# Token tile 0 transposed among tile 1's last matmuls, the next weights converted behind its parts

## The chip, the cores and the metric

The kernel runs on one core of a Trainium2 chip. The metric is the device time of one execution, in microseconds (us). Four engines matter here, each with a queue of its own that it works through in order: TensorE (PE in the profile, its weight loads PEld) multiplies, VectorE (DVE) and ScalarE (ACT) do element-wise work, and SyncE (SP) issues the loads from memory.

## The reference

Two transformer blocks run one after the other on 256 tokens of width 1024, all in float32. Where a block ends one sublayer and begins the next, the same steps come: a full-width projection, an addition to the residual, an RMS norm, and the next projection. Cut to that, the three places of the change are:

```python
# first block, behind the mixer and behind the feed-forward part
x = x + rms_norm(merged @ w_out, norm_mix_post)
h = rms_norm(x, norm_ffn_pre)
u = causal_dwconv(h @ w_up, conv_ffn_w)
...
x = x + rms_norm(f @ w_down, norm_ffn_post)
u = rmsnorm(x, norm_mix_g_2)          # second block begins
proj = u @ w_in_2
...
# second block, behind its mixer
h = x + merged @ w_out_2
hn = rmsnorm(h, norm_mlp_g_2)
y = square(relu(hn @ w_up_2)) @ w_down_2
```

## The kernel before

The 256 tokens lie in two tiles of 128 (`tt` is 0 or 1). A float32 product is made of three matmuls of rounded parts: every operand is split into a high part and the rest (`wh` and `wl` for weights, the two halves of an `Act` tile for activations), and `mm_N` issues high by high, high by rest, and rest by high. The conversion of a weight piece, 128 rows by 1024 numbers, is a cast on ACT (`wh<-raw`, L186) and a subtraction on DVE (`wl<-raw,wh`, L187). The raw pieces come by DMA into four buffers, so a new load is issued when the subtraction four pieces earlier is done.

The program gives an order of work; a scheduler then sets the order of instructions on each engine ahead of the run, and the engines keep to it. `tc.issue_after(i)` binds what is traced inside to stand behind instruction `i` on its engine.

The change concerns three passages from a projection with the tokens in the rows of its result to the next such projection. They are called passage 1 (`w_out` to `w_up`, activations `h2T`), passage 2 (`w_down` to `w_in_2`, `uT`) and passage 3 (`w_out_2` to `w_up_2`, `hnT`). In each:

- `down_tail` finishes the projection: PE fills two PSUM banks for tile 0, then two for tile 1 (`pN`, 48 matmuls for a tile in passages 1 and 3).
- `normed` then works on tile 0: squares of the two banks on ACT, a reciprocal root in small steps on DVE (`rsr`, `rsa` and others), the new residual `x`, its squares, and the normed tile `xm`, in two halves. `to_T` transposes it on PE (`tr`, eight transposes into two banks), and casts on ACT with subtractions on DVE split each bank into two parts of the activations. The same chain of squares, `x` and `xm` follows for tile 1.
- `head_N` multiplies the normed tiles with the first 1024 columns of the next weights, in two halves of 512 columns (`n` 0 and 1), each of four pieces of two `k` each. PE does tile 0 with half 0, tile 0 with half 1 (`pM`, 24 matmuls each), transposes tile 1, and does tile 1 with both halves.

In `head_N` the first `free` pieces of half 0 are converted when the scheduler likes, the others of half 0 behind the last square and the last half of tile 0's `xm` (`normed_`), and all of half 1 behind the last split of tile 0 (`transposed`). `free` is 2 in passages 1 and 2, and 4 in passage 3.

Of the kernel before, what the change touches and what calls it, by code (L numbers as in the profile page):

```python
# [18 lines left out]
P = 128  # L19
# [20 lines left out]
def two_blocks(ctx, tc, ins, out):  # L40
# [240 lines left out]
    def down_tail(banks, w, parts, wts, first, last=False):  # L281
# [17 lines left out]
    def head_N(w, cols, x, ready, done, free=2):  # L299
# [14 lines left out]
    def head_T(w, cols, x, ready, free=2):  # L314
# [6 lines left out]
        head_N(w, cols, x, ready, done, free)  # L321
# [62 lines left out]
    def normed(x, g, dst, mid):  # L384


        xms = []
        for tt in range(NT):
            mid(tt)
            xms.append(norm(x, tt, g))  # L390
            if tt == 0:
                split0 = to_T(dst, 0, xms[0][0])

        def ready(tt):
            if tt:
                to_T(dst, tt, xms[tt][0])

        ready.marks = xms[0][1], split0
        return ready

    def post_norm(x, tt, banks, g):
# [4 lines left out]
        for n in range(2):  # L406
            nc.scalar.activation(sq, banks[n], AF.Square, accum_out=s2[:, n:n + 1])
            nc.vector.tensor_mul(fg[:, n * 512:(n + 1) * 512], banks[n], g[:, n * 512:(n + 1) * 512])
        r = rsqrt([s2[:, 0:1], s2[:, 1:2]], 1.0 / D)
        for n in range(2):  # L410
            cs = slice(n * 512, (n + 1) * 512)
            nc.vector.scalar_tensor_tensor(x[tt][:, cs], fg[:, cs], r, x[tt][:, cs], ALU.mult, ALU.add)

# [209 lines left out]
    def proj_full_N(w, x):  # L623

        banks = [[ps("pN"), ps("pN")] for _ in range(NT)]
        down_tail(banks, w, [(k, x, k) for k in range(KD)], tail_weights(w, 0, 4, tc4), True)
        return banks

    h2 = Act("h2T")

    banks = proj_full_N(ins["w_out"][0], mh)
    ready = normed(xr, g_pre, h2, lambda tt: post_norm(xr, tt, banks[tt], g_post))


    w_up, w_down = ins["w_up"][0], ins["w_down"][0]
    NFH = NF // 2
    def mix(head, at, j0, rest):

        for j, pt in rest:
# [5 lines left out]
            for part, h_ in enumerate(head_T(w_up, (0, D_FF), h2, ready))]  # L645
    banks = [[ps("pN"), ps("pN")] for _ in range(NT)]
# [41 lines left out]
    down_tail(banks, w_down, parts, wts, False)  # L688
    u = Act("uT")
    ready = normed(xr, g_pre, u, lambda tt: post_norm(xr, tt, banks[tt], g_post))  # L690
# [15 lines left out]
    head_N(w2, (OFV, OFV + 512), u, ready,  # L706
# [493 lines left out]
    banks = proj_full_N(ins["w_out_2"][0], mh)  # L1200

# [4 lines left out]
    def add_mix(tt):  # L1206
        for n in range(2):
# [3 lines left out]
    ready = normed(xr, g_mlp, hn, add_mix)  # L1211
# [7 lines left out]
    banks = [[ps("pN"), ps("pN")] for _ in range(NT)]  # L1219
# [11 lines left out]
    down_tail(banks, w_down, parts, wts, False, True)  # L1231
# [30 lines left out]
```

## Time and profile before

| what | value |
|---|---|
| time, median of 3 runs | 929.51 us (928.73 to 929.74) |
| the profiled execution's own time | 929.96 us |
| its span, first to last instruction | 928.2 us |
| PE busy | 907.0 us (98%) |
| DVE busy | 657.0 us (71%) |
| ACT busy | 570.9 us (62%) |

Busy PE is not PE at its peak: a matmul's row lasts longer than the step from one matmul to the next, since they overlap. A bracket at a row's end tells how long its engine had been idle and what ended that.

### The profile page before, as it was taken

How to read it: one execution, taken by the hardware profiler on the slowest of the kernel's cores; microseconds unless marked ns; L12 is line 12 of the kernel's file. 1: busy time of each engine (PE TensorE's matmuls, PEld its weight loads, DVE VectorE, ACT ScalarE, POOL GpSimd, SP SyncE). 2: the span in 40 equal slices, each digit the busy share in tenths (PEclk: the TensorE clock that was granted, in tenths of full speed). 3: DMA queues.
4: the chain of work that ended last, by engine and by line, in shares of the span. 5: the costliest groups of instructions: out<-in, count | busy, mean ns of one | idle time of the engine just before them, and what ended most of it. 6: DMA issues, size and time to landing. Idle time of an engine off the chain costs nothing.

```text
span 928.2 us, 13339 instructions
## 1 busy us (share of the span) xinstructions
PE 907.0 (98%) x4871; PEld 764.0 (82%) x4871; DVE 657.0 (71%) x1152; ACT 570.9 (62%) x989; POOL 73.3 (8%) x127
## 2 busy tenths in 40 slices
PE   6999999999999999999999999999999999999998
PEld 4888788778888888778888768888998788888886
DVE  6557656985888789957989878645688765555553
ACT  5566865564765666647867667754455466556661
POOL 4000000000000000000000189402000000000000
PEclk9999999999999999999999999999999999999999
DMA  7752457456565565663644344544336754556552
GB/s 253 212 157 91 136 182 226 161 172 216 180 214 169 183 193 191 208 201 114 204 137 148 105 134 138 169 137 134 105 123 226 263 167 152 184 180 203 170 164 99
DMA packets 118857, 157.86 MB, mean 170 GB/s; under 512 B 9813, under 2 KB 96072, under 8 KB 118792
## 3 DMA queue, kind: packets, MB, share of 16 engines
q1 hardware_dynamic: 117320, 153.08, 51.6%
q10 hardware_dynamic: 720, 2.62, 0.8%
q0 software_dynamic: 752, 1.31, 0.6%
q8 instruction: 38, 0.62, 0.3%
q14 instruction: 27, 0.22, 0.1%
HBM read 154.11 MB, written 2.88 MB: 169 GB/s over the span
## 4 chain that ended last, share of the span: by engine, by line
PE 84%; DVE 7%; DMA 4%; ACT 3%; issue 1%; SPq 0%; ACTq 0%; DVEq 0%
PE pT L226 30%; PE pT L228 15%; PE pN L264 6%; PE pN L265 6%; PE pN L266 6%; PE pM L264 4%; PE pM L265 4%; PE pM L266 4%; DVE wl L187 3%; PE pS L997 2%; DMA raw<-in_w_out_dram 1%; ACT wh L186 1%; DMA raw<-in_w_in_dram 1%; DMA raw<-in_w_proj_gdn_dram 1%; DMA raw<-in_w_down_dram 1%
## 5 line engine op out<-in xcount | busy, mean ns | idle before, releaser
L187 DVE TENSOR_TENSOR wl<-raw,wh 128x1024 fp32r<-128x1024 f32 x282 | 346.1, 1234 | 101.4 <-PE pT L228 72.8
L186 ACT CAST wh<-raw 128x1024 fp32r<-128x1024 f32 x282 | 290.6, 1050 | 107.1 <-PE pT L226 38.2
L226 PE MATMUL pT<-uT,wh 128*128 128x512 f32 x384 | 102.3, 403 | 0.0
L240 DVE TENSOR_TENSOR py<-py,pT 128x256 f32<-128x256 f32 x136 | 55.9, 416 | 54.7 <-ACT py L239 54.3
L264 PE MATMUL pN<-wh,fTh 128*128 128x512 f32 x216 | 83.9, 393 | 0.5 <-ACT wh L186 0.5
L265 PE MATMUL pN<-wl,fTh 128*128 128x512 f32 x216 | 84.3, 391 | 0.1
L266 PE MATMUL pN<-wh,fTl 128*128 128x512 f32 x216 | 83.9, 390 | 0.0
L239 ACT COPY py<-pT 128x256 f32<-128x256 f32 x136 | 48.8, 370 | 55.0 <-PE pT L228 54.6
L226 PEld LDWEIGHTS pT<-uT,wh 128*128 128x128 f32 x384 | 68.5, 189 | 12.6 <-issue 0.5
L226 PE MATMUL pT<-hT,wh 128*128 128x512 f32 x288 | 73.4, 396 | 0.0
L226 PE MATMUL pT<-h2T,wh 128*128 128x512 f32 x288 | 72.2, 392 | 0.0
L226 PEld LDWEIGHTS pT<-hT,wh 128*128 128x128 f32 x288 | 51.6, 188 | 10.4 <-issue 0.2
L226 PEld LDWEIGHTS pT<-h2T,wh 128*128 128x128 f32 x288 | 52.1, 189 | 9.6
L228 PEld LDWEIGHTS pT<-uT,wl 128*128 128x128 f32 x384 | 52.2, 190 | 3.6
L228 PE MATMUL pT<-uT,wl 128*128 128x256 f32 x384 | 53.8, 282 | 0.0
L264 PEld LDWEIGHTS pN<-wh,fTh 128*128 128x128 f32 x216 | 40.5, 188 | 9.2 <-ACT wh L186 1.4
L226 PE MATMUL pT<-hnT,wh 128*128 128x512 f32 x192 | 47.8, 391 | 0.0
L265 PEld LDWEIGHTS pN<-wl,fTh 128*128 128x128 f32 x216 | 40.6, 188 | 8.6 <-DVE wl L187 0.8
L266 PEld LDWEIGHTS pN<-wh,fTl 128*128 128x128 f32 x216 | 40.6, 188 | 8.4
L228 PEld LDWEIGHTS pT<-hT,wl 128*128 128x128 f32 x288 | 39.3, 190 | 2.8
L228 PEld LDWEIGHTS pT<-h2T,wl 128*128 128x128 f32 x288 | 39.3, 190 | 2.8
L926 POOL DMA_DIRECT2D bm<-scr x1 | 0.8, 775 | 515.7 <-DVE cv L798 515.7
(377 smaller groups left out, 1642.8 us busy)
## 6 DMA issues: line engine op xcount, KB each, us to landing
raw<-in_w_in_dram SPq DMA_DIRECT2D x112, 512.0 KB, 3.6
raw<-in_w_up_dram SPq DMA_DIRECT2D x76, 512.0 KB, 4.6
raw<-in_w_down_dram SPq DMA_DIRECT2D x54, 512.0 KB, 4.2
raw<-in_w_out_dram SPq DMA_DIRECT2D x16, 512.0 KB, 4.0
raw<-in_w_proj_fox_dram SPq DMA_DIRECT2D x8, 512.0 KB, 3.3
raw<-in_w_proj_gdn_dram SPq DMA_DIRECT2D x8, 512.0 KB, 3.6
raw<-in_w_att_branch_dram SPq DMA_DIRECT2D x4, 512.0 KB, 3.6
raw<-in_w_conv_branch_dram SPq DMA_DIRECT2D x4, 512.0 KB, 4.0
```

What stands on the lines that cost most here:

```text
L186: nc.scalar.copy(wh, raw)
L187: nc.vector.tensor_sub(wl, raw, wh)
L226: mm(dst, wt.at(k, cs)[0], x.both(k), start=(k == 0), stop=(k == kt - 1), skip_group_check=True)
L228: mm(dst[:, T:2 * T], wt.at(k, cs)[1], x.at(k)[0], start=False, stop=(k == kt - 1), skip_group_check=True)
L239: nc.scalar.copy(y[:, i, :], pt[:, 0:T])
L240: nc.vector.tensor_add(y[:, i, :], y[:, i, :], pt[:, T:2 * T])
L264: mm(dst, xh, wh, start=first, stop=False)
L265: mm(dst, xh, wl, start=False, stop=False)
L266: mm(dst, xl, wh, start=False, stop=last)
L926: nc.gpsimd.dma_start(bm, scr.rearrange("u b r c -> (u b) r c"))
L997: mm(pt[:, hl, :], *f(hl), start=True, stop=True)
```

## The change

`normed` becomes a class `Norm` whose two steps the projection calls itself. `down_tail` starts tile 0's chain (`start(0)`) ahead of tile 1's matmuls and transposes tile 0 (`turn(0)`) ahead of the last four groups of three matmuls of tile 1; tile 1's chain is started behind them. The conversions of the next weights get other bounds: in passage 1 the first piece of half 0 stands behind tile 0's squares of the banks and its `xm`, the second behind the squares of `x` and the last split of tile 0; in passages 2 and 3 two pieces are free; everything else stands behind tile 0's last split. The first product of `head_N` takes its 24 matmuls in another order: high by high for all eight `k`, then rest by high, then high by rest.

```diff
@@ Wt
-                if behind and len(self.pieces) > behind[0]:
-                    with tc.issue_after(behind[1]), tc.issue_after(behind[2]):
+                after = behind and behind[len(self.pieces) - 1]
+                if after:
+                    with tc.issue_after(after[0]), tc.issue_after(after[1]):
                         self.convert()
@@ down_tail
-            elif last:
+            elif norm is None:
                 order = [(n, q) for n in range(2) for q in both]
             else:
+                norm.start(0)
                 order = [(n, q) for q in both for n in range(2)]
-            for n, (wt, (k, x, xk)) in order:
+            for i, (n, (wt, (k, x, xk))) in enumerate(order):
+                if tt and norm and i == len(order) - 4:
+                    norm.turn(0)
                 mm_N(banks[tt][n], wt, k, x, xk, tt, slice(n * 512, (n + 1) * 512),
                      first and k == parts[0][0], k == parts[-1][0])
+        if norm:
+            norm.start(1)
@@ head_N
-        normed_, transposed = ready.marks
-        wts = [Wt(w, 0, KD, cols[0], 512, tc4, behind=(free, *normed_)),
-               Wt(w, 0, KD, cols[1], 512, None, behind=(0, *transposed))]
+        behind = [None] * free + [norm.early, (norm.late[0], norm.turned[1])][free:] + [norm.turned] * 2
+        wts = [Wt(w, 0, KD, cols[0], 512, tc4, behind=behind),
+               Wt(w, 0, KD, cols[1], 512, None, behind=[norm.turned] * 4)]
         for tt in range(NT):
-            ready(tt)
+            if tt:
+                norm.turn(tt)
             for n in (0, 1) if tt == 0 else (1, 0):
                 pt = pj("pM")
-                for k in range(KD):
-                    mm_N(pt, wts[n], k, x, k, tt, slice(None), k == 0, k == KD - 1)
+                if (tt, n) == (0, 0):
+                    ts = slice(0, P)
+                    for a in range(3):
+                        for k in range(KD):
+                            mm(pt, x.at(k, ts)[a == 1], wts[n].at(k, slice(None))[a == 2],
+                               start=(a == 0 and k == 0), stop=(a == 2 and k == KD - 1))
+                else:
+                    for k in range(KD):
+                        mm_N(pt, wts[n], k, x, k, tt, slice(None), k == 0, k == KD - 1)
                 done(n, tt, pt)
@@ Norm in the place of normed
+        def start(self, tt):
+            act = self.mid(tt)
+            self.xm[tt], marks = norm(self.x, tt, self.g)
+            if tt == 0:
+                self.early, self.late = (act, marks[1]), marks
+
+        def turn(self, tt):
+            marks = to_T(self.dst, tt, self.xm[tt])
+            if tt == 0:
+                self.turned = marks
@@ the calls
-    banks = proj_full_N(ins["w_out"][0], mh)
-    ready = normed(xr, g_pre, h2, lambda tt: post_norm(xr, tt, banks[tt], g_post))
+    banks = pN()
+    to_h2 = Norm(xr, g_pre, h2, lambda tt: post_norm(xr, tt, banks[tt], g_post))
+    proj_full_N(banks, ins["w_out"][0], mh, to_h2)
...
-    heads = head_T(w_up, (0, 512), hn, ready, 4)
+    heads = head_T(w_up, (0, 512), hn, to_hn, 2)
```

`head_T` passes `free` on, and its default goes from 2 to 0 (passage 1); `post_norm` now returns its last square on ACT.

The first place is PE's queue in passage 1, at the end of the projection and the start of the next. In the names, `pN_310` and `pN_311` are tile 1's two banks, `xm_353` is the normed tile 0, `tr_354` and `tr_355` its two transposed banks, `h2T_304` to `h2T_307` the four parts of the activations, `wh_377`, `wh_380`, `wh_383` and `wh_386` the four pieces of half 0, and `wh_389` the first of half 1. Before:

```order
L266 MATMUL pN_311_1737<-wh_334_1782,mT_247_1469 128x512
L379 MATMUL tr_354_1926<-ident_88,xm_353_1923 128x128 x4
L379 MATMUL tr_355_1935<-ident_88,xm_353_1923 128x128 x4
L264 MATMUL pM_400_2038<-wh_377_1992,h2T_304_1730 128x512
L265 MATMUL pM_400_2038<-wl_378_1993,h2T_304_1730 128x512
```

And with the change (between the fourth row and the fifth stand eleven more matmuls into `pN_310` and `pN_311`):

```order
L267 MATMUL pN_311_1737<-wh_328_1770,mT_246_1468 128x512
L393 MATMUL tr_354_1914<-ident_88,xm_353_1875 128x128 x4
L393 MATMUL tr_355_1923<-ident_88,xm_353_1875 128x128 x4
L265 MATMUL pN_310_1736<-wh_331_1776,mT_247_1469 128x512
...
L321 MATMUL pM_400_2038<-wh_377_1992,h2T_304_1730 128x512 x2
L321 MATMUL pM_400_2038<-wh_380_1998,h2T_305_1731 128x512 x2
L321 MATMUL pM_400_2038<-wh_383_2004,h2T_306_1732 128x512 x2
L265 MATMUL pM_401_2064<-wh_389_2016,h2T_304_1730 128x512
L321 MATMUL pM_400_2038<-wh_386_2010,h2T_307_1733 128x512 x2
L321 MATMUL pM_400_2038<-wh_377_1992,h2T_304_1730 128x512 x2
```

The transposes moved up by twelve matmuls, and within its first seven matmuls behind them `pM` now asks for three more pieces, one of them a piece of half 1. Passage 3 reads alike. In passage 2 `tr` moved up by six matmuls, one of which stands between its two banks.

The second place is ACT's queue in passage 1, from tile 0's squares on. Before:

```order
L186 CAST wh_377_1992<-raw_376_1990 128x1024
L407 ACTIVATE sq_337_1883,ss2_336_1882<-pN_308_1734 128x512
L186 CAST wh_380_1998<-raw_379_1996 128x1024
L407 ACTIVATE sq_337_1883,ss2_336_1882<-pN_309_1735 128x512
L365 ACTIVATE sq_346_1906,ss2_345_1905<-x_1_95 128x512 x2
L186 CAST wh_383_2004<-raw_382_2002 128x1024
L186 CAST wh_386_2010<-raw_385_2008 128x1024
L407 ACTIVATE sq_357_1945,ss2_356_1944<-pN_310_1736 128x512
L407 ACTIVATE sq_357_1945,ss2_356_1944<-pN_311_1737 128x512
L122 CAST h2T_304_1730<-tr_354_1926 128x2x128
```

With the change, from the squares of `x` on:

```order
L379 ACTIVATE sq_346_1858,ss2_345_1857<-x_1_95 128x512 x2
L187 CAST wh_380_1998<-raw_379_1996 128x1024
L122 CAST h2T_304_1730<-tr_354_1914 128x2x128
L122 CAST h2T_305_1731<-tr_354_1914 128x2x128
L122 CAST h2T_306_1732<-tr_355_1923 128x2x128
L122 CAST h2T_307_1733<-tr_355_1923 128x2x128
L422 ACTIVATE sq_357_1945,ss2_356_1944<-pN_310_1736 128x512
L187 CAST wh_383_2004<-raw_382_2002 128x1024
L422 ACTIVATE sq_357_1945,ss2_356_1944<-pN_311_1737 128x512
L187 CAST wh_389_2016<-raw_388_2014 128x1024
L187 CAST wh_386_2010<-raw_385_2008 128x1024
```

The casts of pieces 3 and 4 (`wh_383`, `wh_386`) moved from ahead of tile 1's squares to behind them, with `wh_389` between. In passage 2 both squares of tile 1's banks stand ahead of the last cast of an activation part and of the same three casts; in passage 3 piece 3 and the first piece of half 1 stand ahead of tile 1's first square, piece 4 behind it.

The third place is DVE's queue in passage 1, from the additions of tile 1 on (`fg` is a bank times a gain, `x_2` the residual of tile 1). With the change:

```order
L423 TENSOR_TENSOR fg_358_1946<-pN_311_1737,gain_norm_mix_post_242_1462 128x512
L358 TENSOR_SCALAR rsa_363_1955<-ss2_356_1944 128x1
L188 TENSOR_TENSOR wl_384_2005<-raw_382_2002,wh_383_2004 128x1024
L360 SCALAR_TENSOR_TENSOR rsa_364_1957<-ss2_356_1944,rsa_363_1955 128x1
L188 TENSOR_TENSOR wl_387_2011<-raw_385_2008,wh_386_2010 128x1024
L362 TENSOR_SCALAR rsr_359_1951<-rsa_364_1957 128x1
L188 TENSOR_TENSOR wl_390_2017<-raw_388_2014,wh_389_2016 128x1024
L364 SCALAR_TENSOR_TENSOR rsy_362_1954<-rsr_359_1951,rsa_364_1957 128x1
L368 TENSOR_SCALAR rsc_360_1952<-rsr_359_1951 128x1
L188 TENSOR_TENSOR wl_393_2023<-raw_391_2020,wh_392_2022 128x1024
```

Before, `wl_384` and `wl_387` stood ahead of this chain, and `wl_390` and `wl_393` behind the two instructions that make `x_2`. Now four conversions stand inside the steps that lead to `x_2`. The queues of SP and POOL keep their order, but for one load that the store of a residual tile now precedes.

## Rows read from the trace of the kernel before

**Rows 1.** The page: the span, and the chain that ended last by engine.
```profile
span 928.2 us, 13339 instructions
...
PE 84%; DVE 7%; DMA 4%; ACT 3%; issue 1%; SPq 0%; ACTq 0%; DVEq 0%
```

**Rows 2.** Timeline of PE, passage 1: start, duration, instruction, [idle before <-releaser].
```profile
191.66 0.39 PE L264 MATMUL pN<-wh,mT 128*128 128x512 f32 x1
...
199.14 1.03 PE L379 MATMUL tr<-ident,xm 128*128 128x128 f32 x8
200.40 0.50 PE L264 MATMUL pM<-wh,h2T 128*128 128x512 f32 x1 [0.23 <-ACT h2T L122]
200.74 0.39 PE L265 MATMUL pM<-wl,h2T 128*128 128x512 f32 x1
...
212.94 0.50 PE L264 MATMUL pM<-wh,h2T 128*128 128x512 f32 x1
```

**Rows 3.** Timeline of PE, passage 2.
```profile
386.40 1.04 PE L379 MATMUL tr<-ident,xm 128*128 128x128 f32 x8
...
388.81 0.50 PE L266 MATMUL pM<-wh,uT 128*128 128x512 f32 x1 [0.61 <-DVE rsa L344]
...
400.41 1.29 PE L379 MATMUL tr<-ident,xm 128*128 128x128 f32 x8 [0.88 <-DVE xm L370]
401.50 0.49 PE L264 MATMUL pM<-wh,uT 128*128 128x512 f32 x1
```

**Rows 4.** Timeline of PE, passage 3.
```profile
742.25 1.03 PE L379 MATMUL tr<-ident,xm 128*128 128x128 f32 x8
...
755.65 0.50 PE L264 MATMUL pM<-wh,hnT 128*128 128x512 f32 x1
```

**Rows 5.** Timeline of ACT, passage 1.
```profile
188.46 0.60 ACT L407 ACTIVATE sq<-pN 128x512 f32<-128x512 f32 x1 [0.63 <-PE pN L266]
...
195.25 1.98 ACT L186 CAST wh<-raw 128x1024 fp32r<-128x1024 f32 x2
198.66 0.60 ACT L407 ACTIVATE sq<-pN 128x512 f32<-128x512 f32 x1 [1.42 <-PE pN L266]
...
202.64 2.95 ACT L186 CAST wh<-raw 128x1024 fp32r<-128x1024 f32 x3
```

**Rows 6.** Waits of ACT from 198 to 214 us: total, times, longest.
```profile
ACT h2T L122 <- DVE h2T L125: 1.9, 3, 0.8
```

**Rows 7.** Timeline of DVE, passage 1.
```profile
191.26 0.68 DVE L408 TENSOR_TENSOR fg<-pN,gain_norm_mix_post 128x512 f32<-128x512 f32 x1
...
196.60 1.42 DVE L370 SCALAR_TENSOR_TENSOR xm<-x,rsr,gain_norm_ffn_pre 128x512 f32<-128x512 f32 x2
197.93 2.36 DVE L187 TENSOR_TENSOR wl<-raw,wh 128x1024 fp32r<-128x1024 f32 x2
...
203.85 1.41 DVE L412 SCALAR_TENSOR_TENSOR x<-fg,rsr,x 128x512 f32<-128x512 f32 x2
...
210.87 1.41 DVE L370 SCALAR_TENSOR_TENSOR xm<-x,rsr,gain_norm_ffn_pre 128x512 f32<-128x512 f32 x2
```

**Rows 8.** DMA issues by line: size of one, median us to landing.
```profile
raw<-in_w_up_dram SPq DMA_DIRECT2D x76, 512.0 KB, 4.6
```

**Rows 9.** Timeline of ACT, passage 2: the first cast behind the transposes.
```profile
387.04 0.37 ACT L122 CAST uT<-tr 128x256 fp32r<-128x256 f32 x1 [0.44 <-PE tr L379]
```

**Rows 10.** Timeline of DVE, passage 2: tile 0 normed.
```profile
384.73 1.42 DVE L370 SCALAR_TENSOR_TENSOR xm<-x,rsr,gain_norm_mix_g 128x512 f32<-128x512 f32 x2
```

**Rows 11.** Timeline of DVE, passage 3: tile 0 normed, tile 1 added.
```profile
737.14 1.41 DVE L370 SCALAR_TENSOR_TENSOR xm<-x,rsr,ain_norm_mlp_g 128x512 f32<-128x512 f32 x2
...
741.76 1.37 DVE L1209 TENSOR_TENSOR x<-pN,x 128x512 f32<-128x512 f32 x2 [2.08 <-PE pN L266]
```

**Rows 12.** Windows ahead of passage 1: busy us of PE, PEld, DVE, ACT, POOL; granted clock; DMA.
```profile
176.00:179.80 3.80, 1.89 (x7) 1.22 (x7) 3.80 (x7) 2.79 (x4) 0.00 (x0) 1.00 0.29 114
179.90:183.20 3.30, 3.30 (x9) 2.58 (x8) 3.30 (x5) 1.67 (x2) 0.00 (x0) 0.50 0.77 271
```

More of the change, by code (lines that the diff above doesn't have):

```diff
@@ L279, in tail_weights, with down_tail @@
         return [Wt(w, k, 1, 0, D, alloc) for k in range(k0, k1)]
-    def down_tail(banks, w, parts, wts, first, last=False):
+    def down_tail(banks, w, parts, wts, first, norm=None):
         m = len(wts)
@@ L319, in done @@
             nc.scalar.copy(nat[n][:, tt, :], pt)
-        head_N(w, cols, x, ready, done, free)
+        head_N(w, cols, x, norm, done, free)
         def pairs(t):
@@ L382, in to_T, with __init__ @@
         return last
[L384 to L390, printed above, removed]
-            if tt == 0:
[L392 to L399, printed above, removed]
+    class Norm:
+        def __init__(self, x, g, dst, mid):
+            self.x, self.g, self.dst, self.mid, self.xm = x, g, dst, mid, {}
+        def start(self, tt):
+            act = self.mid(tt)
+            self.xm[tt], marks = norm(self.x, tt, self.g)
+            if tt == 0:
+                self.early, self.late = (act, marks[1]), marks
[3 more added lines that the diff above has]
+                self.turned = marks
     def post_norm(x, tt, banks, g):
@@ L406, in post_norm @@
         for n in range(2):
-            nc.scalar.activation(sq, banks[n], AF.Square, accum_out=s2[:, n:n + 1])
+            act = nc.scalar.activation(sq, banks[n], AF.Square, accum_out=s2[:, n:n + 1])
             nc.vector.tensor_mul(fg[:, n * 512:(n + 1) * 512], banks[n], g[:, n * 512:(n + 1) * 512])
@@ L412, in post_norm @@
             nc.vector.scalar_tensor_tensor(x[tt][:, cs], fg[:, cs], r, x[tt][:, cs], ALU.mult, ALU.add)
+        return act.ins
     x_in = ins["x"][0]
@@ L621, in two_blocks, with proj_full_N, pN @@
     mh = merge([(ins["w_att_branch"][0], oh), (ins["w_conv_branch"][0], ch)], sg)
[L623 to L627, printed above, removed]
+    def proj_full_N(banks, w, x, norm):
+        down_tail(banks, w, [(k, x, k) for k in range(KD)], tail_weights(w, 0, 4, tc4), True, norm)
+    def pN():
+        return [[ps("pN"), ps("pN")] for _ in range(NT)]
     h2 = Act("h2T")
-    banks = proj_full_N(ins["w_out"][0], mh)
-    ready = normed(xr, g_pre, h2, lambda tt: post_norm(xr, tt, banks[tt], g_post))
+    banks = pN()
+    to_h2 = Norm(xr, g_pre, h2, lambda tt: post_norm(xr, tt, banks[tt], g_post))
+    proj_full_N(banks, ins["w_out"][0], mh, to_h2)
     w_up, w_down = ins["w_up"][0], ins["w_down"][0]
@@ L644, in two_blocks @@
     gens = [mix(h_, (1, 3), 4, proj_T(w_up, part * D_FF + 512, D_FF - 512, h2))
-            for part, h_ in enumerate(head_T(w_up, (0, D_FF), h2, ready))]
-    banks = [[ps("pN"), ps("pN")] for _ in range(NT)]
+            for part, h_ in enumerate(head_T(w_up, (0, D_FF), h2, to_h2))]
+    banks = pN()
     parts, first = [], True
@@ L687, in two_blocks @@
         parts += [(j + i, fh, o + i) for i in range(2)]
-    down_tail(banks, w_down, parts, wts, False)
     u = Act("uT")
-    ready = normed(xr, g_pre, u, lambda tt: post_norm(xr, tt, banks[tt], g_post))
+    to_u = Norm(xr, g_pre, u, lambda tt: post_norm(xr, tt, banks[tt], g_post))
+    down_tail(banks, w_down, parts, wts, False, to_u)
     w2 = ins["w_in_2"][0]
@@ L705, in two_blocks @@
     fv = [t4("fv", (P, D)) for _ in range(NT)]
-    head_N(w2, (OFV, OFV + 512), u, ready,
+    head_N(w2, (OFV, OFV + 512), u, to_u,
            lambda n, tt, pt: nc.scalar.copy(fv[tt][:, n * 512:(n + 1) * 512], pt))
@@ L1198, in two_blocks @@
     hn = Act("hnT")
-    banks = proj_full_N(ins["w_out_2"][0], mh)
+    banks = pN()
     xr = [t4("x", (P, D)) for _ in range(NT)]
@@ L1209, in add_mix @@
             nc.vector.tensor_add(xr[tt][:, cs], banks[tt][n], xr[tt][:, cs])
-    ready = normed(xr, g_mlp, hn, add_mix)
+    to_hn = Norm(xr, g_mlp, hn, add_mix)
+    proj_full_N(banks, ins["w_out_2"][0], mh, to_hn)
     w_up, w_down = ins["w_up_2"][0], ins["w_down_2"][0]
     NK = D_FF_2 // P
-    heads = head_T(w_up, (0, 512), hn, ready, 4)
+    heads = head_T(w_up, (0, 512), hn, to_hn, 2)
     head = chain(heads[0], ((4 + j, pt) for j, pt in heads[1]))
     gen = mix(head, (1, 3, 5, 7), 8, proj_T(w_up, 1024, D_FF_2 - 1024, hn))
-    banks = [[ps("pN"), ps("pN")] for _ in range(NT)]
+    banks = pN()
     parts, tails, first = [], [], True
@@ L1230, in two_blocks @@
         parts += [(j + i, fh, o + i) for i in range(2)]
-    down_tail(banks, w_down, parts, wts, False, True)
+    down_tail(banks, w_down, parts, wts, False)
     for tt in range(NT):
```

4 lines of the change are left out of this document (2 added, 2 removed).

## The prediction

> **What bounds the kernel now.** I read the page first: the span is 928.2 us, and 84% of the chain that ended last is PE [rows 1]. So I count only what makes PE wait or start later; work of other engines costs nothing until PE stands at it. The profiled execution took 929.96 us, 1.76 us more than its span. It lies 0.45 us above the median of the three runs, 929.51 us, and a difference is added to the median at the end.
>
> Next I read PE's timeline through the three passages and measured each from the first transpose of tile 0 to the first matmul behind tile 1's transposes. They last 212.94 - 199.14 = 13.80 us in passage 1 [rows 2], 15.10 us in passage 2 (386.40 to 401.50) [rows 3] and 13.40 us in passage 3 (742.25 to 755.65) [rows 4]. The work in each is 48 matmuls and 16 transposes. From 191.66 to 199.14 us PE started 33 matmuls, one per 0.227 us [rows 2], so 48 take 10.88 us. Eight transposes last 1.03 us with the tail of the last one, some 0.87 us to the next start [rows 2]. That is 12.62 us of work, and the rest is waiting: 1.18, 2.48 and 0.78 us, together **4.4 us**. This is all that the change can win in these passages. About 1.6 us of it stands at tile 1's transposes (0.9 us in passage 2 for `xm` alone [rows 3]), the rest behind tile 0's.
>
> **The change, part by part.** Nothing is added or removed: the same transposes, squares, casts and subtractions run, in another order. So each part is costed by who waits for it.
>
> *The transposes of tile 0, moved up.* In passage 1 they now come 12 x 0.227 = 2.72 us earlier, at 196.42 us. Tile 0's chain must be done by then. Before, its second `fg` stood behind a conversion and ran at 191.26 us [rows 7]; with the conversion gone it can follow the second square, at about 190.0, so the chain comes 1.26 us earlier and `xm`, before at 196.60 [rows 7], has its halves at 196.05 and 196.75. The two banks are asked for at 196.42 and 196.86: no wait. In passage 3 `xm` was done at 738.55 even before [rows 11], and the transposes come at 739.53: no wait. In passage 2 nothing leaves the chain; the first half of `xm` ends at 384.73 + 0.71 = 385.44 [rows 10], and with a signal's way to PE, put at 0.15 us, PE gets it at 385.6, while it stands at its transposes at 386.40 - 6 x 0.227 = 385.04. So PE waits 0.55 us there, with six matmuls behind it. The projections end at 200.01, 387.87 and 743.12 us, and the 0.5 to 1.3 us of waiting that stood between tile 0's transposes and the next product is gone: the first parts are cast by then.
>
> *The conversions, moved back.* This is where I see the cost. ACT works its queue in order, and the first product takes all eight high parts in its first pass, so PE asks for piece 3 after four matmuls (0.91 us), for a piece of half 1 after six (1.36 us) and for piece 4 after seven (1.59 us). Before, pieces 3 and 4 were cast at 195.25 us, over 3 us ahead of their use, while ACT had nothing else to do [rows 5].
>
> In passage 1 the four casts of the transposed tile now come first. They begin 0.64 us behind the transposes (as 387.04 behind 386.40 in passage 2 [rows 3, 9]). Cast and subtraction of one bank take turns: ACT waited three times for DVE in such a group [rows 6]. So four casts of some 0.37 us with the subtractions between them end at about 199.8, when bank 0 of tile 1 is done too (the square of it started 0.48 us ahead of the projection's end before, 198.66 against 199.14 [rows 2, 5]). From there ACT has a square (0.58 us), piece 3, a square, the piece of half 1, and piece 4, with 1.05 us for a cast or 0.95 us where the next follows at once (2.95 us for three [rows 5]): 199.8 + 0.58 + 1.05 = 201.4 for piece 3, 202.95 for the piece of half 1, 203.9 for piece 4. PE wants piece 4 at 200.01 + 1.59 = 201.6 and gets it at 203.95: **2.35 us of stall**. The last of the three waits also costs the slow start of a matmul behind a wait, 0.34 instead of 0.227 us (200.40 to 200.74 [rows 2]).
>
> In passage 2 both squares and the last cast stand ahead: the three casts end at about 387.65, the squares at 389.0, the last cast at 389.3, and the three pieces at 390.3, 391.25 and 392.2. PE wants the last one at 387.87 + 1.59 = 389.46: **2.8 us**. In passage 3 piece 3 and the piece of half 1 follow the casts at once (743.55 and 744.5), but the square ahead of piece 4 waits for DVE's addition of tile 1. That addition took 0.69 us for a half, at 741.76 before [rows 11]; now it stands behind the four subtractions, its first half ends at 743.7, and behind the cast that ACT is then at, the square ends at 745.0 and piece 4 at 746.05. PE wants it at 744.71: **1.4 us**.
>
> *Tile 1's chain, later.* PE reaches tile 1's transposes 39 matmuls (8.84 us) and a slow start (0.57 us for the last two of the pass) behind the stall, and a few tenths for single subtractions that come late: at 213.45, 401.7 and 755.8. In passage 1, DVE now does four conversions inside the steps to `x`, and the second needs piece 4's cast of 203.9: 203.95 + 3 x 1.14 us (two took 2.36 us [rows 7]) and the small steps give `x` at 208.3 instead of 203.85 [rows 7]. From `x` to `xm` it was 7.02 us with four conversions between [rows 7], now 4.74 us with two. `xm` starts at 213.0; its halves reach PE at 213.9 and 214.6, so PE waits about 0.45 and 0.25 us, and the first matmul behind comes at 215.1 instead of 212.94. In passage 2 the same count gives `x` at 396.05, `xm` at 401.5 with halves at 402.35 and 403.05 for PE, and the matmul at 403.55 instead of 401.50. In passage 3 `xm` is done at 751.8, PE does not wait for it, and the matmul comes at 756.8 instead of 755.65.
>
> *The loads, moved back.* A raw buffer comes free with the subtraction, so four loads in each passage are issued later, by 2 to 10 us in passage 1. A load of `w_up` takes 4.6 us to land [rows 8]. The last piece of half 1 in passage 1 is then asked for at 205.2 and lands at about 209.8; PE needs it at 212.1. This hides behind the matmuls of half 1; without that cover each later piece would cost up to 1 us, which I keep for the range.
>
> **The sum.** 215.1 - 212.94 = 2.2, 403.55 - 401.50 = 2.05, 756.8 - 755.65 = 1.15: together **5.4 us** slower. By the waits, that is 9.8 us against 4.4 us. PE has the same work behind each passage and no idle time that could take this up. 929.96 + 5.4 = 935.4 for the profiled execution, 934.9 from the median; I forecast 935.0.
>
> **The rivals.**
>
> *The conversions keep up* (the other side: faster). If ACT brought piece 4 within the 1.6 us that PE needs to come to it, only the gain would be left: of the 4.4 us of waiting, the part at tile 0 goes, 2.8 us, and the time is 926.7. For it speaks that ACT stood idle for 1.42 us ahead of the square at 198.66 us, and that the same pieces were early before [rows 5]. Against it: two squares and three casts take 4.1 us in a row, the first square can't start before PE has finished bank 0, 0.5 us ahead of the product, and all stand in one queue. It decides where that row shrinks below 2.1 us. Chance 10%.
>
> *Gain and loss cancel.* The waits only change their place, from tile 0's parts to the pieces, and the total stays near 4.4 us: 928 to 931. That takes 4 us off my stalls of 6.6 us. Chance 11%.
>
> *Half of it.* The stall at the pieces is right but tile 1's chain isn't late, or the casts run closer together: 2 to 4 us, 931.5 to 933.5. Chance 17%.
>
> *The clock falls too.* From 179.90 to 183.20 us the granted clock was 0.50, the lower of the two levels, 1.2 GHz, right after a stretch of 3.80 us in which PE was busy for 1.89 us [rows 12]. The stalls of passages 1 and 2 leave PE as idle: some six matmuls in the 3.5 us up to piece 4. At half the clock 3.3 us of work lose some 1.65 us, of which the waits at tile 1 would cover about 0.6: 1 us for each passage, so 936 to 937. The waits at 388.81 and 400.41 us [rows 3] are shorter and didn't bring it down (the matmul behind the second still lasted 0.49 us), so I leave this beside the forecast. Chance 20%. The Trainium skill states such a rule (TensorE: Matmul & The Clock Gate, "HAM oscillation — how this bites in real kernels"): gaps between matmuls throttle the clock anew each time that they come. By that rule it would be 937 here, and the trace agrees with it at 179.90 us.
>
> **How the numbers follow.** The forecast has 42%, with a range of its own of 934.0 to 936.0. Leaving out the two cases at the bottom, about 2 in 10, and reaching to a clock that falls in two passages with loads that come late, I give 931.5 to 938.5. A measurement of this kernel can tell about 0.2%, 1.9 us, from no change. Slower by more: forecast, clock and nearly all of the half case, 78%. Within: 11%. Faster: 11%.
>
> **What would show it.** Right: in each passage PE waits for `wh` in the first pass of `pM`, in passages 1 and 2 also for `xm` at tile 1's transposes, and no longer behind tile 0's; ACT has tile 1's squares between the activation casts and piece 4; the first matmul behind tile 1's transposes comes 2.2, 2.05 and 1.15 us later than before. Wrong: PE meets piece 4 without a wait (then the order on ACT isn't what ends the wait), or waits of this size appear and are made up for later, or the largest new wait is on a load. The forecast fails altogether if the casts behind the transposed parts run while PE still works on the old projection.

## The result and the profile after

The changed kernel takes 935.43 us (median of 5 runs, 934.26 to 938.17) against 929.51 us: 1.0074 times the time of before, with a 95% interval of 1.0059 to 1.0089. The forecast was 935.0 us. The profiled execution took 934.45 us, 1.75 us more than its span. Of the five executions one has a mean granted clock of 1.000 and took 934.26 us; the three at 0.996 took 935.43, 937.77 and 938.17 us. The profiled one, at 0.998, has one fall of the clock. So the median holds falls that the forecast had left beside it, and an execution without any is still 4.75 us slower than before.

The page first: PE's share of the chain that ended last is a point lower than in [rows 1], and ACT's a point higher.

```profile
span 932.7 us, 13331 instructions
...
PE 83%; DVE 7%; ACT 4%; DMA 4%; issue 1%; SPq 0%; ACTq 0%; DVEq 0%
```

Timeline of PE of the changed kernel, passage 1, to be read beside [rows 2]. The transposes of tile 0 now stand without a wait inside the projection, and the first product (L321) starts at 197.89 us without one. Then it waits three times for `wh`: piece 3, the piece of half 1, piece 4.

```profile
194.06 1.25 PE L393 MATMUL tr<-ident,xm 128*128 128x128 f32 x8
...
197.89 1.07 PE L321 MATMUL pM<-wh,h2T 128*128 128x512 f32 x4
199.18 0.73 PE L321 MATMUL pM<-wh,h2T 128*128 128x512 f32 x2 [0.22 <-ACT wh L187]
200.70 0.50 PE L265 MATMUL pM<-wh,h2T 128*128 128x512 f32 x1 [0.79 <-ACT wh L187]
201.65 2.60 PE L321 MATMUL pM<-wh,h2T 128*128 128x512 f32 x10 [0.44 <-ACT wh L187]
...
212.16 1.29 PE L393 MATMUL tr<-ident,xm 128*128 128x128 f32 x8 [0.39 <-DVE xm L384]
213.24 0.50 PE L265 MATMUL pM<-wh,h2T 128*128 128x512 f32 x1
```

Passage 2 (beside [rows 3]) and passage 3 (beside [rows 4]), the same view:

```profile
386.12 0.63 PE L393 MATMUL tr<-ident,xm 128*128 128x128 f32 x4 [0.42 <-DVE xm L384]
...
388.42 1.07 PE L321 MATMUL pM<-wh,uT 128*128 128x512 f32 x4
390.86 0.73 PE L321 MATMUL pM<-wh,uT 128*128 128x512 f32 x2 [1.36 <-ACT wh L187]
391.80 0.49 PE L265 MATMUL pM<-wh,uT 128*128 128x512 f32 x1 [0.22 <-ACT wh L187]
392.75 4.04 PE L321 MATMUL pM<-wh,uT 128*128 128x512 f32 x10 [0.45 <-ACT wh L187]
...
746.51 1.52 PE L321 MATMUL pM<-wh,hnT 128*128 128x512 f32 x6
747.91 0.51 PE L265 MATMUL pM<-wh,hnT 128*128 128x512 f32 x1
749.47 2.59 PE L321 MATMUL pM<-wh,hnT 128*128 128x512 f32 x10 [1.05 <-ACT wh L187]
```

The row at 392.75 us holds ten matmuls in 4.04 us where passages 1 and 3 need 2.60 and 2.59: the clock. Windows of this stretch and the one ahead of it (columns as in [rows 12]):

```profile
388.50:392.70 4.20, 2.22 (x8) 0.97 (x6) 3.86 (x9) 4.17 (x9) 0.00 (x0) 0.98 0.00 0
392.80:396.10 3.30, 3.30 (x8) 2.62 (x9) 3.27 (x8) 1.26 (x2) 0.00 (x0) 0.53 0.77 243
```

What a passage costs is told by its matmuls: the shift of the first matmul behind tile 1's transposes against the same matmul of before, less the shift of a matmul well ahead of tile 0's transposes. Both are found by their number in PE's row, and this leaves out what happens elsewhere. For the changed kernel that is **+2.66, +2.78 and +1.03 us**, together 6.5. Elsewhere the two profiles differ too: ahead of passage 1 the profile of before is 2.4 us longer, with the fall of the clock of [rows 12], which the changed kernel's profile has not. 6.5 less 2.4 is 4.1 of the 4.5 us between the two profiled executions.

ACT's row in passage 1 of the changed kernel shows where the pieces are (beside [rows 5]): tile 1's squares stand around piece 3, and a cast further on waits for its load.

```profile
197.50 0.60 ACT L422 ACTIVATE sq<-pN 128x512 f32<-128x512 f32 x1
...
198.08 1.05 ACT L187 CAST wh<-raw 128x1024 fp32r<-128x1024 f32 x1
199.02 0.61 ACT L422 ACTIVATE sq<-pN 128x512 f32<-128x512 f32 x1
...
199.60 2.00 ACT L187 CAST wh<-raw 128x1024 fp32r<-128x1024 f32 x2
203.58 1.05 ACT L187 CAST wh<-raw 128x1024 fp32r<-128x1024 f32 x1 [1.98 <-DMA raw<-in_w_up_dram]
```

And DVE's row there, beside [rows 7]: from tile 0's `xm` to tile 1's it is now 18.14 us instead of 14.27. Measured against the projection, as above, tile 0's `xm` starts 1.1 us earlier than before and tile 1's 2.75 us later.

```profile
193.12 1.41 DVE L384 SCALAR_TENSOR_TENSOR xm<-x,rsr,gain_norm_ffn_pre 128x512 f32<-128x512 f32 x2
...
204.66 1.23 DVE L188 TENSOR_TENSOR wl<-raw,wh 128x1024 fp32r<-128x1024 f32 x1 [0.41 <-ACT wh L187]
...
206.38 1.42 DVE L427 SCALAR_TENSOR_TENSOR x<-fg,rsr,x 128x512 f32<-128x512 f32 x2
...
211.26 1.41 DVE L384 SCALAR_TENSOR_TENSOR xm<-x,rsr,gain_norm_ffn_pre 128x512 f32<-128x512 f32 x2
```

The same row in passage 2, 16.68 us from `xm` to `xm`:

```profile
385.22 1.41 DVE L384 SCALAR_TENSOR_TENSOR xm<-x,rsr,gain_norm_mix_g 128x512 f32<-128x512 f32 x2
...
401.90 1.41 DVE L384 SCALAR_TENSOR_TENSOR xm<-x,rsr,gain_norm_mix_g 128x512 f32<-128x512 f32 x2
```

Before, it was 14.78 us: it started at 384.73 [rows 10] and ended with

```profile
399.51 1.42 DVE L370 SCALAR_TENSOR_TENSOR xm<-x,rsr,gain_norm_mix_g 128x512 f32<-128x512 f32 x2
```

### The profile page after: what moved, and what is told of

Same layout as the page of the kernel before. It is cut to its first block, busy times and chain, and to the rows that moved or that the text cites. A ratio compares the mean times of both kernels' runs of the same rounds, so it can differ in the third digit from the quotient of the medians.

```text
span 932.7 us, 13331 instructions
## 1 busy us (share of the span) xinstructions
PE 908.2 (97%) x4871; PEld 762.9 (82%) x4871; DVE 657.4 (70%) x1152; ACT 572.3 (61%) x989; POOL 73.3 (8%) x127
## 4 chain that ended last, share of the span: by engine, by line
PE 83%; DVE 7%; ACT 4%; DMA 4%; issue 1%; SPq 0%; ACTq 0%; DVEq 0%
PE pT L227 31%; PE pT L229 16%; PE pN L265 5%; PE pN L266 5%; PE pN L267 5%; PE pM L266 3%; PE pM L265 3%; PE pM L267 3%; DVE wl L188 3%; ACT wh L187 2%; PE pS L1015 2%; DMA raw<-in_w_out_dram 1%; PE pM L321 1%; DMA raw<-in_w_up_dram 1%; DMA raw<-in_w_in_dram 1%
```

## The experiments

The change has three parts that can be had one by one: the transposes of tile 0 moved up (T), the bounds of the conversions (B) and the high-by-high pass of the first product (O). The table holds what each run did to the passages, by the measure above, and its ratio to the kernel before on the same chip (its median there was 929.51 us beside the change, 930.0 to 930.6 us beside the other runs).

| run | passage 1 | 2 | 3 | sum | median, ratio (95%) |
|---|---|---|---|---|---|
| T+B+O, the change | +2.66 | +2.78 | +1.03 | +6.5 | 935.43, 1.0074 (1.0059 to 1.0089) |
| T | +2.55 | +0.07 | -0.48 | +2.1 | 931.77, 1.0013 (1.0002 to 1.0024) |
| T+O | +2.11 | +0.06 | -0.51 | +1.7 | 931.51, 1.0008 (0.9998 to 1.0019) |
| T+B | +3.65 | +2.03 | -0.53 | +5.2 | 935.12, 1.0045 (1.0029 to 1.0061) |
| T+B+O, half 1 later | +2.85 | +1.78 | +0.58 | +5.2 | 934.60, 1.0047 (1.0030 to 1.0064) |
| T, six subtractions left out | +0.35 | -0.73 | -0.48 | -0.9 | 929.62, 0.9987 (0.9978 to 0.9995) |
| T, one free piece | +0.85 | -0.02 | -0.49 | +0.3 | 930.58, 0.9998 (0.9987 to 1.0009) |
| T, one free piece, half 1 late | -0.06 | -0.48 | -0.49 | -1.0 | 928.55, 0.9982 (0.9973 to 0.9990) |

**T alone** (the run `t_alone`):

```diff
-        behind = [None] * free + [norm.early, (norm.late[0], norm.turned[1])][free:] + [norm.turned] * 2
+        behind = [None] * free + [norm.late] * (4 - free)
...
-                if (tt, n) == (0, 0):
+                if False:
...
-    def head_T(w, cols, x, norm, free=0):
+    def head_T(w, cols, x, norm, free=2):
...
-    heads = head_T(w_up, (0, 512), hn, to_hn, 2)
+    heads = head_T(w_up, (0, 512), hn, to_hn, 4)
```

> Only tile 0's transposes are moved; the conversions have the bounds of before (two pieces free in passages 1 and 2, four in passage 3, the others behind tile 0's xm) and the first product takes k by k. Theory A (the loss comes from the row on ACT: conversions behind the parts and tile 1's squares, wanted early by the first product): the 2.8 us of waiting behind tile 0's transposes go and nothing comes in their place, 926.7 us (926.0 to 928.0), PE waits for no wh in the three passages. Theory B (the transposes themselves cost where they now stand, as they interrupt the projection and block the rows of ACT and DVE): 934 to 936, as with the whole change. Theory C (the high-by-high pass of the first product costs by itself): about 927 as well.

It took 931.77 us: not the 926.7 of theory A. PE waits for no `wh`, as expected, but passage 1 is 2.55 us longer all the same. DVE's and PE's rows of that run in passage 1:

```profile
189.00 1.23 DVE L188 TENSOR_TENSOR wl<-raw,wh 128x1024 fp32r<-128x1024 f32 x1 [0.57 <-ACT wh L187]
...
195.48 1.41 DVE L384 SCALAR_TENSOR_TENSOR xm<-x,rsr,gain_norm_ffn_pre 128x512 f32<-128x512 f32 x2
...
207.92 1.42 DVE L427 SCALAR_TENSOR_TENSOR x<-fg,rsr,x 128x512 f32<-128x512 f32 x2
...
211.44 1.42 DVE L384 SCALAR_TENSOR_TENSOR xm<-x,rsr,gain_norm_ffn_pre 128x512 f32<-128x512 f32 x2
```

```profile
196.38 0.63 PE L393 MATMUL tr<-ident,xm 128*128 128x128 f32 x4 [1.41 <-DVE xm L384]
...
212.34 1.40 PE L393 MATMUL tr<-ident,xm 128*128 128x128 f32 x8 [1.70 <-DVE xm L384]
```

The conversion at 189.00 us (of the second piece, as free as before) stands between tile 0's steps to `xm`, so tile 0's moved transposes wait 1.4 us. And the scheduler, which decides anew, has put all four conversions of half 1 ahead of tile 1's `x`, so its transposes wait 1.7 us. In passage 2, T alone changes nothing: `xm` of tile 0 and of tile 1 start 14.86 us apart, in the profile of before 14.78.

```profile
386.65 1.41 DVE L384 SCALAR_TENSOR_TENSOR xm<-x,rsr,gain_norm_mix_g 128x512 f32<-128x512 f32 x2
...
401.51 1.41 DVE L384 SCALAR_TENSOR_TENSOR xm<-x,rsr,gain_norm_mix_g 128x512 f32<-128x512 f32 x2
```

```profile
402.41 1.29 PE L393 MATMUL tr<-ident,xm 128*128 128x128 f32 x8 [0.95 <-DVE xm L384]
```

PE's wait at tile 1's transposes is 0.95 us there, where it was 0.88 [rows 3]; behind tile 0's it waits 0.26 us instead of 0.61, but 0.42 us ahead of them for tile 0's own `xm`. From here on there is a theory D: in passages 1 and 2 DVE's row up to tile 1's `xm` sets the end.

**T and O** (`t_and_order`): the diff above without its `if False`.

> The whole change but the bounds: transposes moved and high-by-high pass first, conversions bound as before. Theory A: pieces 3 and 4 are cast ahead of the parts, so PE finds them; but all four parts are now wanted within 1.6 us, and in passage 2 two squares stand ahead of the last three casts, which costs up to 1 us there: 927.7 us (926.5 to 929). Theory B: 934 to 936. Theory C (the order of the first product is what costs): about 5.9 us slower than the run with the transposes alone, 932 to 934.

931.51 us. The high-by-high pass costs nothing where the pieces are early: within 0.5 us of T in every passage. Theory C falls, and so does B, with passage 3 0.51 us faster.

**T and B** (`t_and_bounds`): only `if (tt, n) == (0, 0)` became `if False`.

> The whole change but the order of the first product, which goes k by k. Theory A: PE wants piece 3 after 12 matmuls and piece 4 after 18, so the stalls at wh go; in passage 1 a smaller one for wl of piece 3 stays (some 0.8 us). But tile 1's chain on DVE stays as late as with the whole change, since its four conversions stand in the same places, and PE then waits 1 to 2.5 us for xm at tile 1's transposes in passages 1 and 2: these passages gain little (0.1 and 0.7 us), passage 3, where xm isn't late, gains 1.2 us: 933.0 us (932.0 to 934.5). Theory C: with the order undone the loss is gone, about 927. Theory B: 934 to 936.

935.12 us, 0.45% over before, or 4.2 us where theory A had 3.5. The stalls at `wh` are gone but for one of 0.3 us, and passages 1 and 2 stay long: PE now waits for `wl` and, at 213.44 and 404.02 us, for `xm`. Passage 1 lost 1.0 us against the change where 0.1 us of gain had been expected: ACT waited 2.97 us for the load of a piece, and DVE's fourth conversion 1.40 us for that cast.

```profile
204.87 1.05 ACT L187 CAST wh<-raw 128x1024 fp32r<-128x1024 f32 x1 [2.97 <-DMA raw<-in_w_up_dram]
```

Passage 2 gained 0.75 us, as expected in size, but the clock didn't fall in this profile, so that the gain is not the order's alone. In passage 3 the loss is gone: +1.03 with B and O, -0.48, -0.51 and -0.53 without one or both. There it takes both, the late casts and the pass that asks for them early, as the prediction had it.

**Half 1 later** (`half1_later`):

```diff
-                nc.scalar.copy(wh, raw)
+                self.last = nc.scalar.copy(wh, raw).ins
...
-        wts = [Wt(w, 0, KD, cols[0], 512, tc4, behind=behind),
-               Wt(w, 0, KD, cols[1], 512, None, behind=[norm.turned] * 4)]
+        wts = [Wt(w, 0, KD, cols[0], 512, tc4, behind=behind)]
+        wts.append(Wt(w, 0, KD, cols[1], 512, None, behind=[(wts[0].last, norm.turned[1])] * 4))
```

> The whole change, but the first piece of half 1 is bound behind the cast of piece 4, so that ACT does piece 4 right behind piece 3 (and a square), and the matmul of half 1 inside the first product goes behind it. Theory A: piece 4 comes 0.95 us earlier in each passage, and PE's last stall is shorter by that; in passage 1 the end doesn't move, as xm for tile 1 is as late as before; passage 2 gains up to 0.9 us, and 1.4 us more in executions where the clock then doesn't fall; passage 3 gains 1.0 us: 933.6 us (932.5 to 935). If the stalls at the pieces alone set the ends of the passages: 3 us less, 932.4. Theory B: no change, 935.4.

934.60 us. Passage 1 didn't gain (+2.85), passage 2 gained 1.0 us, passage 3 only 0.45 where I expected 1.0 (tile 1's first square still stands ahead of piece 4). That a shorter stall gives passage 1 nothing says that its end isn't set by the stall: PE waits 0.55 us for `xm` behind it. The 1.0 us of passage 2 can't be put down to the stall either. The clock did not fall there in this profile (the ten matmuls last 2.57 us, not 4.04), and PE waits 0.55 us for `xm` at the end.

```profile
392.73 2.57 PE L321 MATMUL pM<-wh,uT 128*128 128x512 f32 x10 [0.21 <-ACT wh L187]
```

**Subtractions given to GpSimd** (`t_pool`, `before_pool`, `after_pool`): T, the kernel before and the changed kernel with

```diff
-                nc.vector.tensor_sub(wl, raw, wh)
+                (nc.gpsimd if len(self.pieces) - 1 in self.pool else nc.vector).tensor_sub(wl, raw, wh)
...
-               Wt(w, 0, KD, cols[1], 512, None, behind=[norm.turned] * 4)]
+               Wt(w, 0, KD, cols[1], 512, None, behind=[norm.turned] * 4, pool=(2, 3))]
```

> As the run with tile 0's transposes alone moved, and the subtraction of the last two pieces of half 1 is done by GpSimd, in all three passages. Theory D (new: passages 1 and 2 end when tile 1's xm is there, and this is paced by DVE's row from tile 0's xm on, which holds four conversions inside the steps to x_2, so that waits of PE removed at tile 0 come back at tile 1): two conversions of 1.14 us leave that row, xm comes some 2.3 us earlier in passage 1 and 1.1 us in passage 2; PE's waits at tile 1's transposes (1.9 and 1.05 us) go: 928.9 us (928.0 to 930.0), if GpSimd needs no more than some 2 us for a piece; at 4 us PE waits for these pieces in half 1 instead and the gain is lost. Theory E (the transposes cost by breaking the projection, not by DVE): no change against that run, 931.8.

> The kernel before, with the subtraction of the last two pieces of half 1 on GpSimd. Theory D: DVE's row is shorter by two conversions here too, and the 1.6 us of waiting at tile 1's transposes go, but those behind tile 0's stay: 929.0 us (928.0 to 930.0) against 930.5, so that the run with the transposes moved is then no slower. Theory E: no change, 930.5.

> The whole change, with the subtraction of the last two pieces of half 1 on GpSimd. Theory A (in the changed kernel PE's stalls at wh set the ends of the passages): only the wait for xm in passage 1 goes, 0.5 us; 934.8 us (934.0 to 935.5). Theory D alone (DVE's row sets them): about 2 us less in passage 1 and 1 us in passage 2: 932.5 us.

All three were slower: 938.98, 937.91 and 941.61 us, 1.0093, 1.0082 and 1.0112 times before. DVE's row wasn't relieved. GpSimd's two pieces in passage 1 of T, and DVE's row beside them:

```profile
204.47 5.60 POOL L189 TENSOR_TENSOR wl<-raw,wh 128x1024 fp32r<-128x1024 f32 x2 [192.07 <-ACT wh L188]
```

```profile
205.36 2.39 DVE L370 SCALAR_TENSOR_TENSOR rsq<-rsy 128x1 f32<-128x1 f32 x1
207.78 2.31 DVE L371 SCALAR_TENSOR_TENSOR rsq<-rsq,rsy 128x1 f32<-128x1 f32 x1
210.12 0.16 DVE L372 SCALAR_TENSOR_TENSOR rsr<-rsq,rsc 128x1 f32<-128x1 f32 x1
```

Steps of one column that take 0.16 us elsewhere last 2.39 and 2.31 us, until GpSimd is done with a piece. So these runs say nothing for or against theory D.

**The kernel before again** (`before_again`), nothing changed:

> The kernel before, profiled in another execution, to tell what of the difference ahead of passage 1 is the kernel's. There the profile of before reaches the projection 2.4 us later than the changed kernel's, with the granted clock at 0.50 from 179.9 to 183.2 us. If that fall is chance, this profile has none there or elsewhere, and the stretch takes about 2 us less; if it belongs to the kernel, it is there again.

928.53 us. The passages are within 0.09 us of the first profile's, which is how far the table can be trusted. Ahead of passage 1 it is 2.8 us shorter, without the fall of the clock:

```profile
176.00:179.80 3.80, 3.33 (x14) 2.57 (x15) 3.80 (x5) 1.69 (x3) 0.00 (x0) 1.00 0.54 160
179.90:183.20 3.30, 3.30 (x16) 2.68 (x15) 2.86 (x3) 1.66 (x2) 0.00 (x0) 1.00 0.84 272
```

**Subtractions left out** (`t_skip`, `after_skip`): T and the changed kernel with

```diff
-                nc.vector.tensor_sub(wl, raw, wh)
+                if len(self.pieces) - 1 not in self.skip:
+                    nc.vector.tensor_sub(wl, raw, wh)
```

and `skip=(2, 3)` for half 1.

> As the run with the transposes alone moved, but the subtractions of the last two pieces of half 1 are left out in the three passages (the low parts of the first two pieces are used in their place, so six of the 282 subtractions are missing and the result is not the reference's). No engine takes them over. Theory D (passages 1 and 2 end with tile 1's xm, paced by DVE's row): xm comes at least 1.1 us earlier in both, the waits of 1.9 and 1.05 us at tile 1's transposes go: 928.9 us (928.0 to 930.0) against 931.8. Theory E (the moved transposes cost by themselves): 931.5, no change.

> The whole change, with the same six subtractions left out. Theory A (in the changed kernel PE's stalls at the pieces set the ends of the passages): only the wait of 0.5 us for xm in passage 1 goes, 934.8 us (934.0 to 935.5). Theory D alone (DVE's row sets them): passages 1 and 2 are shorter by 2 and 1 us, 932.5.

T without them took 929.62 us, 2.2 us less than T: passage 1 went from +2.55 to +0.35, passage 2 from +0.07 to -0.73, passage 3 kept its -0.48. All of passage 2's gain and 1.2 us of passage 1's are DVE's row from `xm` to `xm`, shorter by 0.79 and 1.22 us, as theory D has it. The other 1.0 us of passage 1 is an `xm` of tile 0 that came earlier, ahead of everything that was left out; why is not shown. (Without its subtraction a raw buffer is free as soon as it is cast, so loads can move as well.) With the whole change it took 939.35 us, 1.0099 times before (1.0078 to 1.0121), *more* than the changed kernel, which neither theory said. In passage 1 the scheduler had filled the place with the subtraction of a later weight, ahead of `xm`, and a load came later:

```profile
205.63 1.05 ACT L191 CAST wh<-raw 128x1024 fp32r<-128x1024 f32 x1 [2.60 <-DMA raw<-in_w_up_dram]
```

```profile
212.68 1.23 DVE L193 TENSOR_TENSOR wl<-raw,wh 128x1024 fp32r<-128x1024 f32 x1
213.82 1.41 DVE L389 SCALAR_TENSOR_TENSOR xm<-x,rsr,gain_norm_ffn_pre 128x512 f32<-128x512 f32 x2
```

So DVE's row there wasn't shorter: 19.26 us from `xm` to `xm`. PE's stalls at the pieces were those of the changed kernel, within 0.01 us, and PE then waited 2.01 us for `xm`; passage 1 was +3.8. So there `xm` sets the end of passage 1, as D has it, but what a shorter row would win in the changed kernel the run doesn't tell. The clock fell behind that wait, and again in passage 2 (+3.2), as in the changed kernel. Only its passage 3, at +1.00, is clear: with less to do for DVE it is as long as with the change (+1.03), since there ACT's casts set the end.

**T with late pieces of half 1, and with one free piece alone** (`t_late_half1`, `t_free1`): T with `free=1` in passage 1, and, in the first of the two runs, also

```diff
+        late = [norm.turned] * 2
+        if free < 4:
+            late = [(norm.turned[0], post_norm.last)] * 2
...
-               Wt(w, 0, KD, cols[1], 512, None, behind=[norm.turned] * 4)]
+               Wt(w, 0, KD, cols[1], 512, None, behind=[norm.turned] * 2 + late)]
...
+        post_norm.last = dve.ins
```

so in passages 1 and 2 (`dve` is the last of the two instructions that make tile 1's `x`).

> The transposes moved, the first product k by k, and the bounds set by theory D: in passage 1 only the first piece of half 0 is free (the second no longer stands between the steps to tile 0's xm), and in passages 1 and 2 the last two pieces of half 1 stand behind the new residual of tile 1 on DVE, as two of them did in passage 1 before. Theory D: in passage 1 the wait of 1.6 us at tile 0's transposes goes and xm for tile 1 comes some 1 us earlier against tile 0's, so it ends 0.5 us ahead of before instead of 2.55 us behind; passage 2 about 0.5 us ahead, passage 3 0.5 us as in the run with the transposes alone: 929.0 us (928.0 to 930.5) against 930.4 for the kernel before and 931.8. Theory E: 931 to 932.

> The run with late pieces of half 1 without their lateness: one free piece in passage 1, but all four conversions of half 1 again ahead of x_2 on DVE (three in passage 2). Theory D: in passage 1 the wait at tile 0's transposes goes as there, but tile 1's xm is late by the two conversions that stand ahead of x_2, some of them hidden: PE waits 2 to 3 us at tile 1's transposes, the passage ends 1.5 to 2.5 us behind before instead of 0.06 ahead, and passage 2 is at +0.07 as with the transposes alone; 931.0 us (930.3 to 932). If it was the second piece alone that cost in passage 1 (and the wait at tile 0 what it paid), this run is as fast as that one, 928.6.

928.55 us with both: 0.9982 of before (0.9973 to 0.9990), so a little faster than both kernels, and 930.58 us with the free piece alone. Theory E falls: the transposes stand as in T. On DVE the two runs differ, in passage 1, only in where two conversions stand. Rows of `t_late_half1`:

```profile
193.28 1.41 DVE L387 SCALAR_TENSOR_TENSOR xm<-x,rsr,gain_norm_ffn_pre 128x512 f32<-128x512 f32 x2
...
203.83 1.42 DVE L430 SCALAR_TENSOR_TENSOR x<-fg,rsr,x 128x512 f32<-128x512 f32 x2
205.16 1.22 DVE L188 TENSOR_TENSOR wl<-raw,wh 128x1024 fp32r<-128x1024 f32 x1
206.36 1.22 DVE L188 TENSOR_TENSOR wl<-raw,wh 128x1024 fp32r<-128x1024 f32 x1
...
208.71 1.41 DVE L387 SCALAR_TENSOR_TENSOR xm<-x,rsr,gain_norm_ffn_pre 128x512 f32<-128x512 f32 x2
```

And of `t_free1`:

```profile
193.08 1.42 DVE L384 SCALAR_TENSOR_TENSOR xm<-x,rsr,gain_norm_ffn_pre 128x512 f32<-128x512 f32 x2
...
205.89 1.41 DVE L427 SCALAR_TENSOR_TENSOR x<-fg,rsr,x 128x512 f32<-128x512 f32 x2
...
209.41 1.42 DVE L384 SCALAR_TENSOR_TENSOR xm<-x,rsr,gain_norm_ffn_pre 128x512 f32<-128x512 f32 x2
```

The conversions at 205.16 and 206.36 us fill the time in which DVE would wait for ACT's squares of `x`; ahead of `x` they are in the way. That is worth 0.9 us in passage 1 and 0.46 in passage 2. The free piece alone was worth 1.7 us (+2.55 to +0.85), where I had expected 1.05 us at most: an `xm` of tile 0 that starts at 193.08 instead of 195.48 us (0.3 us of it was there before) starts the whole row earlier. So theory D needs both ends, where the row starts and what stands in it.

**Where the passages end.** Read through all eight runs of the table, the first matmul behind tile 1's transposes starts 1.98 or 1.99 us behind tile 1's `xm`: in passage 1 in every one, in passage 2 in every one but the changed kernel (2.89 us, where the stall and the clock end last). In passage 2 tile 0's `xm` starts at the same time in all of them against the projection, within 0.01 us, so the length of DVE's row from `xm` to `xm` alone gives the passage: it is 14.78 us before, 14.86 in T, 16.82 in T+B and 14.31 with late pieces of half 1.

## Why the prediction was right, and where it was not

**The transposes of tile 0.** As predicted: no wait in passages 1 and 3. In passage 2 they start 0.58 us behind the end of the matmul ahead of them (385.31 + 0.23 to 386.12 us); the prediction said 0.55.

**The stalls at the pieces.** As predicted, row by row. From the projection's end to piece 4, less 1.59 us of matmuls, it is 2.17 us in passage 1 (197.89 to 201.65), 2.74 us in passage 2 (388.42 to 392.75) and 1.37 us in passage 3 (746.51 to 749.47). The prediction had 2.35, 2.8 and 1.4.

**Tile 1's chain.** In passage 1 `x` was to come at 205.9 us (208.3 less the 2.36 us by which this profile is ahead there); it came at 206.38. The reason that was given, piece 4's cast, came out: the cast ends at 201.60 us and DVE takes the piece at 201.63, where 201.59 was forecast (its conversion ahead of it ends then too). What came on top is a wait in DVE's row for the *fourth* conversion, whose piece came late from memory (the cast at 203.58 us waited 1.98 us for its load). The step that failed is "This hides behind the matmuls of half 1". The loads asked for later do reach PE, by way of DVE's row. The forecast put this at nothing, it is 0.5 us, and makes the passage +2.66 instead of +2.2; in T+B the same wait was 1.40 us.

**Passage 2 and the clock.** The forecast of +2.05 became +2.78 because the rival of the clock came true there, at 0.53 for 3.3 us. It cost about 1.6 us (the shift against before grows from 2.68 to 4.27 us over these matmuls), and PE then met no wait at tile 1's transposes, where it had been forecast to stand from 401.7 to 402.35 us: about half was covered, as the rival said. So the sign that PE waits for `xm` in passage 2 did not show. In passage 1, with PE nearly as idle, the clock stayed up.

**Passage 3:** +1.03 against +1.15.

**What the forecast got wrong is what it took for granted.** "This is all that the change can win in these passages", 4.4 us, and with it the rival at 926.7 us for conversions that keep up. With T and T+O they do keep up, no `wh` is waited for, and the time is 931.5 to 931.8. The waits behind tile 0 were no price of their own in passages 1 and 2: PE waited there for parts and still arrived at tile 1's transposes no later than the last half of `xm`. Taken away, they come back as waits for `xm` of one tile or the other. Only in passage 3, where `xm` has time to spare, do they turn into a gain, 0.5 us.

So what the forecast named as the cost is the cost: T+O and the change differ in the bounds of the conversions alone, and take 1.0008 and 1.0074 times before. But it works through two rows, and the stalls on ACT that the forecast put first set the end only in part.

- In passage 3 it is the casts on ACT together with the order of the first product.
- In passage 2 the bounds are the cause: +0.07 us without, +2.0 with them. DVE does six conversions between tile 0's `xm` and tile 1's either way, but in T two of them fill the time in which DVE would wait for the transposes. Bound behind the parts they come later, and from `xm` to `xm` it is 16.68 us instead of 14.86.
- In passage 1 the stall of 2.2 us is real, but without it (T, T+O) the passage is nearly as long, by a later `xm` of tile 0 and a longer row than before. In the changed kernel the two limits lie close together: by the stalls PE comes to tile 1's transposes 2.14 us later than before (211.61 us), and then it stands another 0.55 us until `xm` is there. So taking away the stall alone wins nothing there, and a shorter row alone at most 0.75 us (the 0.55 and 0.20 us between the halves of `xm`), by these rows. What the conversions in DVE's row and the late load have of it one by one isn't settled: the run meant to tell (`after_skip`) brought in another subtraction.

That 935.43 us lies so near the forecast is in part luck. The passages cost 6.5 us where 5.4 were forecast, 0.5 more by the load and 0.7 more by the clock, and the fall of the clock ahead of passage 1, which had lengthened the profile of before, is not in the changed kernel's.

## What to carry to other kernels

A wait that is removed is only won if nothing else is due at the same time later: before a wait is counted as gain, look at the next place where the waiting engine meets the others, and at when they will be there. Here that was a row of DVE that the move of PE's work didn't shorten. And where a scheduler orders the instructions, moving one thing re-sorts others: a low-priority conversion that slips between the small steps of a chain costs its whole length, unless it is bound to a place where the chain waits for another engine anyway.

## What the hardware showed that was not expected

- A DVE instruction of one column with two inputs from SBUF stood for 2.39 us (0.16 elsewhere) while GpSimd subtracted a 128x1024 piece, which took 2.70 us on average (6 of them) against DVE's 1.22. The Trainium skill (SBUF — State Buffer, "SBUF: two separate sides") says that the two engines share a port pair and that the one that comes second is blocked for the whole instruction; the trace agrees.
- The granted clock fell to 0.50, the lower level, behind a stretch of passage 1 in T, in which PE was busy for 2.06 of 3.80 us, as it did in passage 2 of the changed kernel behind 2.22 of 4.20. It did not behind 2.34 of 3.80 us in passage 1 of the changed kernel:

```profile
197.90:201.70 3.80, 2.34 (x9) 1.09 (x7) 3.80 (x8) 3.70 (x7) 0.00 (x0) 1.00 0.54 172
```

  In T this cost 1.46 us more than the table's passage 1 says (+4.01 behind it). The same stretch of an unchanged kernel, ahead of passage 1, fell in one execution and not in another.
